# Last rows' norm scaled by a diagonal on TensorE, and an earlier start of the parameter loads, in a two-layer hybrid decoder kernel

## The chip, the cores and the metric

The kernel runs on one core of one Trainium2 chip. The metric is the device time in microseconds (us) of one execution, taken as the median of several runs. Engines are called by their names: TensorE (PE in the rows, PEld for its weight loads), VectorE (DVE), ScalarE (ACT), GpSimd (POOL) and SyncE (SP). DMAs are issued from the queues of SP, ACT and POOL.

## The reference

Two decoder layers work on x of 256 rows and 2048 columns, float32. Each layer multiplies x by one wide input matrix, feeds the product's column groups to three token mixers (a short convolution, latent attention with rotary positions, an RWKV-7 recurrence), concatenates their gated outputs and applies an output projection, a residual and a LayerNorm:

```python
for l in range(DEPTH):
    u = x @ w_in[l]
    (cb, cc, ch, cg, cq, ckv, kpe, mg, rcols, rg) = _split(u, IN_SIZES)
    ...
    mix = jnp.concatenate([y_conv, y_mla, y_rwkv], axis=-1)
    x = _layer_norm(DEEPNORM_ALPHA * x + mix @ w_out[l], ln_g[l], ln_b[l])
```

Here x is the input (1, 256, 2048), and the result has the same shape.

## The kernel before

**Arithmetic.** A float32 operand that feeds a large product is split into a high part (a cast on ScalarE) and a low part (a subtraction on VectorE), both in the type fp32r, and the product is summed from two or three fp32r matmuls. A few smaller products use plain float32 operands.

**Order.** The code emits the work group by group: for each layer the column groups of the input product in the order k, a, r, v, cq, cc and so on, then the attention products, then the output projection `out_proj`. The mixers are generators; `tick()` advances each of them by a step between blocks of a group's matmuls, so that their small instructions run beside TensorE's matmuls. A scheduler at compile time fixes each engine's order by simulated ready times and priorities; `after(a, b)` only says that a stands behind b in an engine's order. On the chip each engine runs its list in that order.

**The first group.** For layer 0 the group k is special (`wide_group`, `load_first`): x and the weights of k come together, in the blocks that `STEPS` lists as (first chunk, number of chunks) of the 16 chunks of 128 rows. Before, the blocks are 1, 1 and then seven times 2 chunks. A chunk is 384 KB. Each block is one DMA on SP's queue into a buffer named `first`, is split into high and low parts of x and of the weights, and gives 12 matmuls for each chunk into the accumulator `u_k`. Buffers of the kind that `first` uses are nine, and four of them hold x.

**Parameters.** `load_constants` starts the DMAs of the parameters `pars`, the constants `cs`, the positions and the matrix of ones on POOL's queue. They stand behind a one-element copy on GpSimd that reads a block of x, so that they start when that block has landed: before, the last one (k0 == 14). `load_params` (line 248) works out `pc` from `pars` with four small VectorE instructions for each layer. The step `shift_mix` (line 472) of the RWKV mixer needs `pc`: four times a ScalarE activation and a VectorE instruction read a quarter of the accumulator `u_k` and write `kx`.

**The second group.** Group a follows: eight blocks of weights `w_a` (4 chunks each), four for the accumulator `u_a` of half 0 and four for that of half 1. Accumulators come from `acc` (line 353), a pool of two buffers in PSUM. `u_k` and the first half of `u_a` hold both; the second half takes the one that the compile-time scheduler expects to be free first. The first half of `u_a` is evicted by a ScalarE copy and a VectorE addition (lines 455 and 456). `rope_tables` (line 262) makes sine and cosine tables from the positions meanwhile, with `Sin` activations on ScalarE.

**The output projection.** `out_proj` computes four groups g of 512 columns, for two halves h of 128 rows. The fourth group is computed in two parts i of 256 columns; in layer 0 the part i = 1 does h = 0, then `add` (VectorE reads the accumulator), then h = 1. Then `root(1)` works out the rows' `rstd` and the mean term, `turn_row` transposes the latter on TensorE (`cwt`, copied to `ct`), and `norm` adds the product of `ct` and `gr` (line 1295, `lw`) with one VectorE instruction for each group and starts the output DMA. In the last layer, groups 1, 2, 3 of the last 128 rows end the kernel. `keep_warm` gives TensorE twelve matmuls whose result nobody reads while VectorE works out `rstd`.

Of the kernel before, what the change touches and what calls it, by code (L numbers as in the profile page):

```python
# [10 lines left out]
F32 = mybir.dt.float32  # L11
# [6 lines left out]
P = 128  # L18
# [93 lines left out]
def hybrid_layers(ctx: ExitStack, tc: tile.TileContext, x, positions, xT, w_in, w_out, w_uq, w_ukv, par, wa_in, gb_in,  # L112
# [34 lines left out]
    def after(inst, earlier):  # L147

        tc.add_manual_dep(inst.ins, earlier.ins.name,
                          mybir.DependencyInfo(mybir.DependencyClass.NoSync, mybir.DependencyReason.DATA),  # L150
                          reason="loads no earlier than needed")
# [15 lines left out]
    def load_constants(x):  # L167

        last = G.tensor_copy(pars[0:1, 0, 0:1], x[0:1, 0:1])
        for to, src in ((pars, par), (cs, cst), (posi, positions[0:1, :].to_broadcast([P, S]))):  # L170
            load = nc.gpsimd.dma_start(to, src)
            after(load, last)
            last = load
        o32 = c4("ones32", (P, 2 * P))
        load = nc.gpsimd.dma_start(o32, sums)
        after(load, last)
        V.tensor_copy(ones, o32)
        loaded.append(load)

    def zeros(rows):  # L180

# [31 lines left out]
    xres = x  # L213
    xs = [pair(f"x0_{g}") for g in range(4)]

    STEPS = [(0, 1), (1, 1), (2, 2), (4, 2), (6, 2), (8, 2), (10, 2), (12, 2), (14, 2)]

    def load_first(k0, n):

        t = s8(f"first{k0}", (P, n, S + 512))  # L220
        in_turn(1, nc.sync.dma_start(t, xT[:, k0:k0 + n, :]))
        with tc.high_priority():
            to, at = xs[k0 // 4], k0 % 4
            split_in(to[:, 0, at:at + n, :], to[:, 1, at:at + n, :], t[:, :, 0:S])
        if k0 == 14:
            load_constants(t[:, 0, :])
        return t[:, :, S:].rearrange("p k (i c) -> p i k c", i=2)

# [19 lines left out]
    def load_params(l):  # L248
        pq = pars[:, l, :]
        pc = cp.tile([P, 29], F32, tag=f"pc{l}", name=f"pc{l}")  # L250
        V.tensor_scalar(pc[:, 0:13], pq[:, Q_MUR:Q_MUR + 13], -1.0, 1.0, ALU.mult, ALU.add)
        V.tensor_scalar(pc[:, 13:21], pq[:, Q_W0:Q_W0 + 8], 0.5, None, ALU.mult)
        V.tensor_scalar(pc[:, 21:25], pq[:, Q_KA:Q_KA + 4], 0.5, None, ALU.mult)
        V.tensor_scalar(pc[:, 25:29], pq[:, Q_KA:Q_KA + 4], -0.5, 1.0, ALU.mult, ALU.add)
        col = lambda j: pq[:, j:j + 1] if j < NQ else pc[:, j - NQ:j - NQ + 1]
        return dict(col=col, om=NQ - Q_MUR, hw=NQ + 13, ha=NQ + 17, hk=NQ + 21, ok=NQ + 25)

# [955 lines left out]
    def ln_rows(l):  # L1213

        t = sm.tile([P, 2, 16], F32, tag="lnp", name=f"lnp{l}", bufs=1)
        load = nc.gpsimd.dma_start(t, gbp[l])
        after(load, loaded[0])
        hi = sm.tile([P, 2, 16], F32R, tag="lnh", name=f"lnh{l}", bufs=1)
        lo = sm.tile([P, 2, 16], F32R, tag="lnl", name=f"lnl{l}", bufs=1)
        V.tensor_copy(hi, t)  # L1220
        V.tensor_tensor(lo, t, hi.bitcast(F32), ALU.subtract)
        rows = dr.tile([5, D], F32R, tag=f"lnr{l}", name=f"lnr{l}")
        for i, src in enumerate((hi[:, 0], lo[:, 0], hi[:, 0], hi[:, 1], lo[:, 1])):
            nc.gpsimd.dma_start(rows[i].rearrange("(p i) -> p i", p=P), src)
        return rows

    def out_proj(l, ms, xres, last, begin, lnr):
# [23 lines left out]
        def rows(g):  # L1251
            return xn[0, :, g * 512:(g + 1) * 512].rearrange("(h p) c -> p h c", p=P)
# [89 lines left out]
        for g in range(4):  # L1342
            xr = c4(f"xr{l}_{g}", (P, 2, 512))
            after(nc.scalar.dma_start(xr, xres[0, :, g * 512:(g + 1) * 512].rearrange("(h p) c -> p h c", p=P)), begin)
            zs.append(xr)
            gt = s4(f"gb{l}_{g}", (P, 2, 512))
            after(nc.scalar.dma_start(gt, gb_in[l:l + 1, :, g * 512:(g + 1) * 512].to_broadcast([P, 2, 512])), begin)
            gs.append(gt)
            if g < 3:
                pa = acc(f"po{l}_{g}")  # L1350
                po = [pa[:, h, :] for h in range(2)]
                for k0 in ORDER:
                    ws = [weights(f"wo{l}_{g}", k0 + k) for k in (0, 2)]
                    for h in range(2):
                        part(po, h, 512, ws)
                for h in range(2):
                    add(po[h], g, 0, 512, h, g)
                continue
            po, held = [], {}
            for i in range(2):  # L1360
                pa = acc(f"po{l}_{g}_{i}")
                po.append([pa[:, h, 0:256] for h in range(2)])
                held[i] = []
                for k0 in ORDER:
                    held[i].append(weights(f"wo{l}_3_{i}", k0))
                    if not last and i == 0:
                        for h in range(2):
                            part(po[i], h, 256, held[0][-1:])
                if not last and i == 0:
                    for h in range(2):  # L1370
                        add(po[i][h], g, 0, 256, h, 3)
            cts = []

            def turn_row(h):
                ct, m = row(h)
                cts.append(ct)
                return m

            first_rows = {AT[last][0]: lambda: turn_row(0),
                          AT[last][1]: lambda: [norm(0, g_, cts[0])[0] for g_ in range(4 if last else 1)][-1]}  # L1380
            for h in range(2):
                for i in range(2):
                    if not last and i == 0:
                        continue
                    part(po[i], h, 256, held[i], first_rows if h and i else {})
                    add(po[i][h], g, i * 256, 256, h, 3 + i)
                mark.setdefault(l + 1, []).append(root(h))
            if not last:
                xs += [pair(f"x{l + 1}_{g}") for g in range(1, 4)]
            keep_warm()  # L1390
            if last:
                turn_row(1)
                part1(256, 256)
                nc.scalar.dma_start(rows(0)[:, 1], zs[0][:, 1])
                for g_ in range(1, 4):
                    norm(1, g_, cts[1], ((0, 512),) if g_ < 3 else ((0, 256), (256, 256)))
            else:
                turn(1, 0, ((0, 2),))
                t = turn(0, 0, hold=mark[l + 1][1])
                after(part0(256, 256), mark[l + 1][1])  # L1400
                mark[l + 1][1] = t
                part1(256, 256)
                nc.gpsimd.dma_start(rows(0), zs[0])
                turn(1, 0, ((2, 2),))
                turn_row(1)
                run(rest(cts))
                tick()
# [60 lines left out]
```

## Time and profile before

| | us |
|---|---|
| median of 3 runs | 908.29 (908.03 to 909.82) |
| the profiled execution, its own time | 909.28 |
| its span in the trace | 907.5 |
| TensorE busy in the span | 893.1 |
| VectorE, ScalarE, GpSimd busy | 687.5, 486.1, 24.6 |

The profiled execution is one more execution beside the three. Its time is 1.8 us longer than the span, which runs from the first to the last event of the trace. Times in the rows count from the start of the span. "Busy" for TensorE holds pipelined matmuls, so 98% is not 98% of its peak rate; it says only that it was seldom without work.

### The profile page before, as it was taken

How to read it: one execution, taken by the hardware profiler on the slowest of the kernel's cores; microseconds unless marked ns; L12 is line 12 of the kernel's file. 1: busy time of each engine (PE TensorE's matmuls, PEld its weight loads, DVE VectorE, ACT ScalarE, POOL GpSimd, SP SyncE). 2: the span in 40 equal slices, each digit the busy share in tenths (PEclk: the TensorE clock that was granted, in tenths of full speed). 3: DMA queues.
4: the chain of work that ended last, by engine and by line, in shares of the span. 5: the costliest groups of instructions: out<-in, count | busy, mean ns of one | idle time of the engine just before them, and what ended most of it. 6: DMA issues, size and time to landing. Idle time of an engine off the chain costs nothing.

```text
span 907.5 us, 16003 instructions
## 1 busy us (share of the span) xinstructions
PE 893.1 (98%) x6314; PEld 786.7 (87%) x6314; DVE 687.5 (76%) x1166; ACT 486.1 (54%) x752; POOL 24.6 (3%) x47
## 2 busy tenths in 40 slices
PE   8899999999999999999999999999999999999996
PEld 8788888888889888888898888888888998988896
DVE  7677988986558987476775889799765699875665
ACT  6577546444447666544246874564444575765430
POOL 2120000000000000000020000000000000000000
PEclk9989999999999999999999999999999999999999
DMA  9755674666535654696576456646654456547832
GB/s 373 222 139 161 185 208 130 187 197 177 161 111 165 193 161 118 205 325 204 171 225 194 136 190 191 170 124 204 196 173 141 123 158 209 163 118 239 315 119 93
DMA packets 65100, 164.98 MB, mean 182 GB/s; under 512 B 15286, under 2 KB 23782, under 8 KB 65014
## 3 DMA queue, kind: packets, MB, share of 16 engines
q1 hardware_dynamic: 57264, 150.36, 54.4%
q10 hardware_dynamic: 5072, 9.57, 3.0%
q0 software_dynamic: 2688, 4.03, 1.6%
q8 instruction: 49, 0.80, 0.4%
q14 instruction: 27, 0.22, 0.1%
HBM read 158.61 MB, written 5.32 MB: 181 GB/s over the span
## 4 chain that ended last, share of the span: by engine, by line
PE 95%; DVE 2%; ACT 1%; DMA 1%; issue 0%; DVEq 0%; SPq 0%; ACTq 0%
PE po L341 7%; PE u_mg L441 7%; PE po L343 7%; PE po L342 6%; PE u_a L441 4%; PE u_cc L441 3%; PE u_cg L441 3%; PE u_mg L443 3%; PE u_v L441 3%; PE u_cb L441 3%; PE u_ch L441 3%; PE u_cq L441 3%; PE u_rg L441 3%; PE u_r L441 3%; PE u_rg L443 2%; PE u_cg L443 2%
## 5 line engine op out<-in xcount | busy, mean ns | idle before, releaser
L138 DVE TENSOR_TENSOR lo_wo<-w_wo,hi_wo 128x1024 fp32r<-128x1024 f32 x57 | 69.1, 1222 | 45.0 <-ACT hi_wo L138 44.1
L138 ACT CAST hi_wo<-w_wo 128x1024 fp32r<-128x1024 f32 x57 | 59.3, 1050 | 60.1 <-PE po L343 29.9
L441 PE MATMUL u_mg<-x,hi_mg 128*128 128x512 f32 x256 | 90.0, 396 | 0.0
L443 PE MATMUL u_mg<-x,lo_mg 128*128 128x256 f32 x256 | 71.4, 280 | 0.0
L441 PEld LDWEIGHTS u_mg<-x,hi_mg 128*128 128x128 f32 x256 | 47.9, 188 | 10.8
L441 PE MATMUL u_a<-x,hi_a 128*128 128x512 f32 x128 | 48.1, 415 | 3.1 <-DVE u_a L138 3.1
L443 PEld LDWEIGHTS u_mg<-x,lo_mg 128*128 128x128 f32 x256 | 48.3, 189 | 0.2
L341 PE MATMUL po<-hi_wo,ma 128*128 128x512 f32 (+1 forms) x128 | 46.7, 365 | 0.0
L343 PE MATMUL po<-hi_wo,ma 128*128 128x512 f32 (+1 forms) x128 | 46.5, 363 | 0.0
L342 PE MATMUL po<-lo_wo,ma 128*128 128x512 f32 (+1 forms) x128 | 46.4, 363 | 0.0
L138 ACT CAST hi_mg<-w_mg 128x1024 fp32r<-128x1024 f32 x32 | 33.6, 1049 | 23.8 <-PE u_mg L441 12.5
L441 PE MATMUL u_cc<-x,hi_cc 128*128 128x512 f32 x128 | 46.2, 403 | 0.0
L441 PE MATMUL u_cg<-x,hi_cg 128*128 128x512 f32 x128 | 46.0, 401 | 0.0
L441 PE MATMUL u_cq<-x,hi_cq 128*128 128x512 f32 x128 | 45.4, 395 | 0.0
L441 PE MATMUL u_ch<-x,hi_ch 128*128 128x512 f32 x128 | 45.3, 399 | 0.0
L441 PE MATMUL u_cb<-x,hi_cb 128*128 128x512 f32 x128 | 45.3, 399 | 0.0
L441 PE MATMUL u_v<-x,hi_v 128*128 128x512 f32 x128 | 45.3, 399 | 0.0
L441 PE MATMUL u_rg<-x,hi_rg 128*128 128x512 f32 x128 | 45.3, 394 | 0.0
L441 PE MATMUL u_r<-x,hi_r 128*128 128x512 f32 x128 | 45.1, 394 | 0.0
L138 DVE TENSOR_TENSOR lo_mg<-w_mg,hi_mg 128x1024 fp32r<-128x1024 f32 x32 | 38.8, 1222 | 6.0 <-ACT hi_mg L138 4.4
L343 PE MATMUL u_k<-x,lo_k 128*128 128x256 f32 x128 | 36.9, 288 | 0.8 <-DVE lo_k L138 0.8
L138 DVE TENSOR_TENSOR lo_rg<-w_rg,hi_rg 128x1024 fp32r<-128x1024 f32 x16 | 19.6, 1223 | 23.2 <-ACT hi_rg L138 23.2
(417 smaller groups left out, 2819.5 us busy)
## 6 DMA issues: line engine op xcount, KB each, us to landing
w_wo<-in_w_out_dram SPq DMA_DIRECT2D x64, 512.0 KB, 4.3
w_mg<-in_w_in_dram SPq DMA_DIRECT2D x32, 512.0 KB, 4.0
w_a<-in_w_in_dram SPq DMA_DIRECT2D x16, 512.0 KB, 4.5
w_r<-in_w_in_dram SPq DMA_DIRECT2D x16, 512.0 KB, 3.7
w_v<-in_w_in_dram SPq DMA_DIRECT2D x16, 512.0 KB, 3.7
w_cq<-in_w_in_dram SPq DMA_DIRECT2D x16, 512.0 KB, 3.8
w_cc<-in_w_in_dram SPq DMA_DIRECT2D x16, 512.0 KB, 4.0
w_ch<-in_w_in_dram SPq DMA_DIRECT2D x16, 512.0 KB, 3.7
```

The costliest lines, as they stand in the source:

```text
L138: inst = call(*args, **kwargs)
L341: m = T.matmul(o, lh, rh, start=first, stop=False, skip_group_check=True)
L342: T.matmul(o, lh, rl, start=False, stop=False, skip_group_check=True)
L343: T.matmul(o, ll, rh, start=False, stop=last, skip_group_check=True)
L441: T.matmul(ps[:, b, :].rearrange("p (i t) -> p i t", i=2), hi[:, k, c], x2, start=k0 + k == 0, stop=False, skip_group_check=True)
L443: T.matmul(ps[:, b, 0:S], lo[:, k, c], x2[:, 0, :], start=False, stop=k0 + k == NKC - 1, skip_group_check=True)
```

## The change

The change has four parts. (1) `STEPS` splits the block of chunks 2 and 3 into two blocks of one chunk. (2) The parameter loads hang on the block that begins at chunk 6 in place of the last one; the cast of the ones moves into `load_params`, and the small instructions of `load_params` are put behind the low part of the last block of k in VectorE's order. (3) In layer 0's output projection, half h = 1 of the part i = 1 gets an accumulator of its own. (4) In the last layer, groups 1 and 2 of the last rows are scaled by TensorE: ScalarE writes a 128x128 diagonal of `rstd`, a float32 matmul multiplies it by the rows, the product of `ct` and `gr` is added in the same PSUM buffer, and ScalarE copies the sum to SBUF. Group 3 is done as before, now ahead of them. The queues of three output DMAs change.

```diff
@@ load_constants
-        V.tensor_copy(ones, o32)
-        loaded.append(load)
+        loaded.extend((load, o32))
@@ blocks of the first group
-    STEPS = [(0, 1), (1, 1), (2, 2), (4, 2), (6, 2), (8, 2), (10, 2), (12, 2), (14, 2)]
+    STEPS = [(0, 1), (1, 1), (2, 1), (3, 1), (4, 2), (6, 2), (8, 2), (10, 2), (12, 2), (14, 2)]
@@ load_first
-        if k0 == 14:
+        if k0 == 6:
             load_constants(t[:, 0, :])
@@ load_params
-        V.tensor_scalar(pc[:, 0:13], pq[:, Q_MUR:Q_MUR + 13], -1.0, 1.0, ALU.mult, ALU.add)
...
+        vs = [V.tensor_scalar(pc[:, 0:13], pq[:, Q_MUR:Q_MUR + 13], -1.0, 1.0, ALU.mult, ALU.add),
...
+        if l == 0:
+            vs.append(V.tensor_copy(ones, loaded[1]))
+        for v in vs:
+            after(v, splits[len(STEPS) - 1][1])
@@ ln_rows
-        V.tensor_copy(hi, t)
+        after(V.tensor_copy(hi, t), splits[len(STEPS)][1])
@@ out_proj, the fourth group
                 pa = acc(f"po{l}_{g}_{i}")
-                po.append([pa[:, h, 0:256] for h in range(2)])
+                pb = pa if last or i == 0 else acc(f"po{l}_{g}_2")
+                po.append([pa[:, 0, 0:256], pb[:, 1, 0:256]])
@@ out_proj, the end of the last layer
             if last:
+                diag = sm.tile([P, P], F32, tag="rs", name="diag", bufs=2)
+                A.activation(diag, ident, AF.Identity, scale=rstd[:, 1:2])
+                scaled = []
+                for g_ in (1, 2):
+                    scaled.append(pm.tile([P, 512], F32, tag="m", name=f"zr{g_}"))
+                    T.matmul(scaled[-1], diag, zs[g_][:, 1, :], start=True, stop=False)
                 turn_row(1)
                 part1(256, 256)
-                nc.scalar.dma_start(rows(0)[:, 1], zs[0][:, 1])
-                for g_ in range(1, 4):
-                    norm(1, g_, cts[1], ((0, 512),) if g_ < 3 else ((0, 256), (256, 256)))
+                nc.sync.dma_start(rows(0)[:, 1], zs[0][:, 1])
+                norm(1, 3, cts[1], ((0, 256), (256, 256)))
+                for g_, pw in enumerate(scaled, 1):
+                    T.matmul(pw, cts[1], gr[:, g_ * 512:g_ * 512 + 512], start=False, stop=True)
+                    z = zs[g_][:, 1, :]
+                    A.copy(z, pw)
+                    (nc.scalar if g_ == 1 else nc.sync).dma_start(rows(g_)[:, 1], z)
```

## Rows read from the trace of the kernel before

**Rows 1.** Waits of TensorE, whole span: us in total, times, longest.

```profile
PE u_a L441 <- DVE u_a L138: 3.1, 1, 3.1
...
PE po L341 <- DVE xr L138: 0.5, 1, 0.5
```

**Rows 2.** TensorE's timeline around 41 us: start, us, engine, line, operation, idle before.

```profile
41.13 0.28 PE L443 MATMUL u_a<-x,lo_a 128*128 128x256 f32 x1
44.49 0.79 PE L441 MATMUL u_a<-x,hi_a 128*128 128x512 f32 x1 [3.08 <-DVE u_a L138]
```

**Rows 3.** Windows: stretch, length, busy per engine, granted clock, DMA share, GB/s.

```profile
44.00:50.00 6.00, 5.51 (x17) 4.74 (x18) 2.33 (x5) 4.51 (x9) 4.69 (x9) 0.50 0.60 124
...
30.27:59.42 29.15, 26.07 (x133) 22.34 (x132) 20.39 (x45) 20.38 (x29) 8.24 (x15) 0.88 0.66 166
482.40:505.84 23.44, 23.44 (x134) 20.27 (x133) 15.87 (x22) 17.53 (x29) 0.00 (x0) 1.00 0.62 180
```

**Rows 4.** VectorE's timeline, 32 to 45 us.

```profile
32.47 0.68 DVE L138 TENSOR_SCALAR pc<-pars 128x13 f32<-128x13 f32 x8
...
44.35 0.48 DVE L138 SCALAR_TENSOR_TENSOR kx<-u_k,pars,kx 128x255 f32<-128x255 f32 x1
```

**Rows 5.** ScalarE's timeline, 30 to 45 us (layer 0).

```profile
30.25 1.05 ACT L138 CAST hi_a<-w_a 128x1024 fp32r<-128x1024 f32 x1 [2.06 <-PE u_k L342]
...
33.80 0.47 ACT L138 ACTIVATE kx<-u_k,pc 128x256 f32<-128x256 f32 x1
...
42.28 0.58 ACT L138 COPY u_a<-u_a 128x512 f32<-128x512 f32 x1
...
43.65 1.28 ACT L138 ACT_TABLE_LOAD   x1
44.95 0.51 ACT L138 ACTIVATE sinT<-ang,cs 128x256 f32<-128x256 f32 x1
```

**Rows 6.** ScalarE's timeline at the same place in layer 1.

```profile
482.39 1.05 ACT L138 CAST hi_a<-w_a 128x1024 fp32r<-128x1024 f32 x1 [1.83 <-PE u_k L342]
483.34 0.47 ACT L138 ACTIVATE kx<-u_k,pc 128x256 f32<-128x256 f32 x1
```

**Rows 7.** Timeline of all engines, 7 to 10 us.

```profile
7.04 0.62 ACT L138 CAST x<-first 128x512 fp32r<-128x512 f32 x1 [0.97 <-DMA first<-in_xT_dram]
...
8.93 0.62 ACT L138 CAST x<-first 128x512 fp32r<-128x512 f32 x1 [0.31 <-DMA first<-in_xT_dram]
...
9.93 0.19 PEld L343 LDWEIGHTS u_k<-x,lo_k 128*128 128x128 f32 x1 [0.96 <-DVE lo_k L138]
```

**Rows 8.** GpSimd's timeline at 18 us.

```profile
18.40 0.93 POOL L169 COPY pars<-first 1x1 f32<-1x1 f32 x1 [3.56 <-DMA first<-in_xT_dram]
```

**Rows 9.** DMA queues, 10 to 28 us: queue, packets, MB, share.

```profile
q0 software_dynamic: 256, 0.70, 10.7%
...
ones<-in_sums_dram POOLq DMA_DIRECT2D x1, 128.0 KB, 6.3
```

**Rows 10.** TensorE's timeline at 316 us: float32 matmuls, two records each.

```profile
316.10 0.38 PE L1092 MATMUL sc<-kn,qn 128*128 128x128 f32 x2
316.32 0.39 PE L1094 MATMUL sc<-kpe,qp 128*128 128x128 f32 x2
```

**Rows 11.** Timeline of all engines from 899 us to the end.

```profile
899.07 0.16 DVE L138 SCALAR_TENSOR_TENSOR rstd<-nr,rstd 128x1 f32<-128x1 f32 x1
...
900.15 0.27 PE L1286 MATMUL cwt<-cs,cw 128*5 128x128 f32 x1 [0.99 <-DVE cw L138]
...
901.07 0.96 PE L1295 MATMUL lw<-gr,ct 5*128 5x512 f32 x4 [0.65 <-DVE ct L138]
901.60 2.19 DVE L138 SCALAR_TENSOR_TENSOR xr<-xr,rstd,lw 128x512 f32<-128x512 f32 x4 [0.59 <-PE lw L1295]
902.38 1.38 SPq L1298 DMA_DIRECT2D out_dram<-xr  x2
```

**Rows 12.** Windows at the end, columns as in rows 3.

```profile
903.20:905.40 2.20, 0.00 (x0) 0.00 (x0) 0.59 (x2) 0.00 (x0) 0.00 (x0) 0.65 0.99 354
```

More of the change, by code (lines that the diff above doesn't have):

```diff
@@ L250, in load_params @@
         pc = cp.tile([P, 29], F32, tag=f"pc{l}", name=f"pc{l}")
-        V.tensor_scalar(pc[:, 0:13], pq[:, Q_MUR:Q_MUR + 13], -1.0, 1.0, ALU.mult, ALU.add)
-        V.tensor_scalar(pc[:, 13:21], pq[:, Q_W0:Q_W0 + 8], 0.5, None, ALU.mult)
-        V.tensor_scalar(pc[:, 21:25], pq[:, Q_KA:Q_KA + 4], 0.5, None, ALU.mult)
-        V.tensor_scalar(pc[:, 25:29], pq[:, Q_KA:Q_KA + 4], -0.5, 1.0, ALU.mult, ALU.add)
+        vs = [V.tensor_scalar(pc[:, 0:13], pq[:, Q_MUR:Q_MUR + 13], -1.0, 1.0, ALU.mult, ALU.add),
+              V.tensor_scalar(pc[:, 13:21], pq[:, Q_W0:Q_W0 + 8], 0.5, None, ALU.mult),
+              V.tensor_scalar(pc[:, 21:25], pq[:, Q_KA:Q_KA + 4], 0.5, None, ALU.mult),
+              V.tensor_scalar(pc[:, 25:29], pq[:, Q_KA:Q_KA + 4], -0.5, 1.0, ALU.mult, ALU.add)]
+        if l == 0:
+            vs.append(V.tensor_copy(ones, loaded[1]))
+        for v in vs:
+            after(v, splits[len(STEPS) - 1][1])
         col = lambda j: pq[:, j:j + 1] if j < NQ else pc[:, j - NQ:j - NQ + 1]
```

## The prediction

> **What bounds the kernel now.** I read the waits of TensorE first, then the timeline around the longest of them, then windows over the same stage in both layers, and last the head and the tail. TensorE is busy 893.1 of 907.5 us, so a change can win in two ways only: by taking away one of TensorE's few waits, or by shortening the stretch after its last large matmul. The waits are a short list [rows 1]: one of 3.1 us before a matmul of `u_a`, one of 0.5 us in `po`, and a shorter one in the first group, which the timeline shows [rows 7]. All other engines work in TensorE's shadow.
>
> The longest wait is at 41.41 us, when the first half of `u_a` is done (41.13 + 0.28), and the second half begins at 44.49 [rows 2]. It needs one of the two accumulators. `u_k` is held until `kx` has read its last quarter, at 44.83 (44.35 + 0.48) [rows 4]; the first half of `u_a` is evicted a little earlier, and that releases TensorE. So `kx` is late. The reason stands in the order of VectorE and ScalarE: `pc` is worked out at 32.47 [rows 4], after which the first `kx` follows at 33.80, 3.55 us after the cast of the fourth `w_a` block at 30.25 [rows 5]. In layer 1, where `pc` has long been there, the same `kx` starts 0.95 us after the same cast (482.39, 483.34) [rows 6], one block earlier, and no wait for `u_a` stands there: there is one in the whole run [rows 1].
>
> The wait costs more than itself. During the idle stretch the granted clock falls to 0.50, the lower level of 1.2 GHz, and stays there through 44 to 50 us [rows 3]. The whole stage from the first matmul of `u_a` to `u_r` takes 29.15 us in layer 0 and 23.44 in layer 1, with TensorE busy throughout the latter at clock 1.00 [rows 3]: 5.7 us more for the same matmuls, 3.1 of them idle and 2.6 by the clock.
>
> **Part 1, smaller blocks.** The block of chunks 2 and 3 lands at 7.04, the next at 8.93 [rows 7]: 1.9 us for two chunks. Its low weights are ready only for the matmul at 9.93, which cost 0.96 us [rows 7]. From there to 30.27 TensorE does 166 matmuls of the group (192 less 26), 0.12 us each, so 1.45 us for a chunk. Split in two, chunk 2 lands half a block earlier, at about 6.1, and its split of half the size (some 1.5 us in place of the 2.9 from 7.04 to 9.93) is over by 7.7; TensorE asks for it at about 9.0. Chunk 3 lands at 7.04, is split by about 8.8 and asked for at 10.4. The block after it still lands at 8.93 and is split by 11.8, as before, just when TensorE, no longer held up, comes to its low part (11.9). So the gain is the whole 0.9, or 0.7 if that meeting misses. One more DMA on SP's queue costs nothing as long as the queue is ahead of the data, and it is: the casts wait for bytes, not for an issue.
>
> **Part 2, parameters.** Moved are the one-element copy (0.93 us on GpSimd) [rows 8], five DMAs on POOL's queue, four `pc` instructions for each layer and the cast of the ones. The copy now waits for the block at chunk 6, one behind that at chunk 4, so it runs at about 8.93 + 1.9 = 10.8 in place of 18.40, 7.6 us earlier. The DMAs follow, and the slowest row takes 6.3 us to land [rows 9], so all are there by about 20 us even with their issues in a row. The DMAs pass the last four blocks of x on SP's queue: 0.70 MB [rows 9], at the rate of the blocks (0.79 MB in 1.9 us) 1.7 us of delay at most. What hides it: a block of two chunks takes 2.9 us of matmuls and 1.9 us to land, so TensorE falls behind the data by 1 us a block. The block at chunk 10, the first that the DMAs can hold up, would be split by about 17.4 and is asked for at about 20.3. I cost the delay at nothing; without that cover it would be 1.7.
>
> `pc` then stands on VectorE behind the last low part of k, at about 21 us, and its eight instructions (0.68) [rows 4] fall into VectorE's idle time there. Queued behind them are the low parts of `w_a`, the first of which TensorE needs at about 29.4. With `pc` ready, `kx` can follow the fourth cast of `w_a` as in layer 1, one block (2.8 us) earlier. That frees `u_k` at about 44.83 - 2.8 - 0.9 = 41.1, against the end of the first half of `u_a` at 41.41 - 0.9 = 40.5: by layer 0's own pace 0.6 of waiting remains, and in layer 1 none does. I take layer 1's stage as the model, 29.15 down to 23.44, a gain of 5.7, less 0.2 for a remainder: 5.5. From both sides: nothing, if the order of `kx` does not move, and 5.7; if it moves, 5.1 to 5.7.
>
> **A table load in the way.** ScalarE loads a table set at 43.65 in 1.28 us, and the `Sin` follows at 44.95, 0.02 after it [rows 5]. With the positions there earlier, the scheduler may put this `Sin` between the third and the fourth `kx`, where it would hold `kx` up by 1.28 + 0.51 = 1.8 us. The Trainium skill, ScalarE: Activation LUTs, What ACT_TABLE_LOAD costs, has a switch of sets at 1283 ns for the load and about 1380 ns for a drain, 2.66 us in all. This trace agrees with the load and shows no drain beside it. By the page the hold-up would be 3.2 us and eat most of the 5.5.
>
> **Part 3, an accumulator of its own.** The wait of 0.5 us in `po` [rows 1] is TensorE's first matmul of h = 1, held by VectorE's reading of h = 0 from the same tile, and the code has one such place. With two tiles nothing is read there. The pool's other buffer is free by then, since the part i = 0 was added before. Gain 0.5 (0.3 if the new tile waits for something else).
>
> **Part 4, the tail.** `rstd` is ready at 899.23 [rows 11]. The diagonal has 128 columns; 256 take 0.47 on ScalarE [rows 5]; I take 0.4, so 899.7. The two matmuls are plain float32. No row has one of 512 columns. One of 128 is two records, and the next begins 0.22 later [rows 10]; four times that is 0.88, and 1.76 for both. From below, four `lw` matmuls in fp32r, 1536 columns, span 0.96 [rows 11], so 0.25 for a pass over 512 and 1.0 for four records; from above, 3.5 at the lower clock. I take 1.76, the same type. TensorE is then free at 901.45, and the transpose `cwt`, behind them in the program, moves from 900.15 to there, 1.3 later. `lw` followed 0.92 after `cwt`, partly because VectorE was busy then; with 0.6 it starts at 902.05, not 901.07. VectorE's first instruction came 0.53 after `lw` [rows 11], now at about 902.6. There the change takes off: VectorE does only group 3, about 0.85 of the 2.19 us, and ScalarE copies the two sums at 0.58 each [rows 5], from about 902.9 to 904.0. But the end is a matter of bytes: the first store, issued at 902.38, flows from 903.20, and the stores then run at 354 GB/s until 905.40 [rows 11, 12]. The same 0.79 MB starts at about 903.05 + 0.8 and needs its 2.2 us again, ending at 906.0. I price the part at +0.6. It is -0.1 if the scheduler puts `cwt` between the two matmuls, and +1.2 if ScalarE's store of group 3's second part stands between its copies and makes the last one wait.
>
> **Sum.** -0.9 - 5.5 - 0.5 + 0.6 = -6.3 us. The profiled execution took 909.28 (span 907.5 and 1.8 around it), so it would be 903.0; it lies 1.0 above the median of the runs, 908.29, so the median would be 902.0. With each term at its ends (5.1 to 5.7 for part 2) the net is -7.2 to -4.9: 901.1 to 903.4.
>
> **Rivals.** *The wait shrinks but stays.* The `Sin` with its table goes ahead of the fourth `kx`, or the scheduler again gives the second half of `u_a` the buffer of the first, which needs a copy of 0.58 and an addition before it is free. Then 1.5 to 3.3 us of the 5.5 remain: 903.5 to 905.3. For it speaks that in layer 1 `kx` and TensorE meet with nothing to spare, and layer 0 has the rope tables besides; against it, that ScalarE and VectorE both have idle stretches between the blocks of `w_a`. *The parameters don't matter.* If the simulated order leaves `kx` behind the fifth cast, the wait and the clock remain, and only 0.9 + 0.5 - 0.6 = 0.8 is won: 907.5. Against it: `pc` stands in the order where its data came, and the data come 7.6 us earlier. *Slower.* The nine small VectorE instructions now stand ahead of all low parts of `w_a`. If the loads on POOL's queue land late behind x, VectorE stops there. It decides from the point where they land after about 28 us: TensorE needs the first low part at 29.4, and it takes 1.2. Each us beyond costs one, and an idle stretch like that of [rows 2] brings the lower clock, 2.6 more; the later wait would be spared. Landing at 34 gives 5.8 + 2.6 on top of the forecast: 910.4. Against it: the slowest landed 6.3 us after its issue with the same queue full [rows 9].
>
> **Chances.** The forecast 0.56, the shrunken wait 0.25, no effect of the parameters 0.14, slower 0.05. A measurement here can tell about 0.2%, 1.8 us, from no change. The first two are faster by more than that (0.81), the third is within it (0.14), the last beyond it (0.05). The range takes in the forecast with its ends and the shrunken wait: 900.9 to 905.3. The forecast's own is 901.1 to 903.4.
>
> **What the profile would show.** Right: no wait of `u_a` on VectorE above 0.5 us and a granted clock of 1.00 from 35 to 60 us; `pc` near 21 us and the first `kx` within 1 us of the fourth cast of `w_a`; no wait near 9.9 and 442 us; the two float32 matmuls taking 1.7 to 1.8 us ahead of `cwt`, and the last bytes about 2.3 us after the first store of group 3 begins to flow. Wrong: `kx` still one block late, a table load between two `kx`, or a wait of VectorE on a DMA near 21 us.

## The result and the profile after

| | before | after |
|---|---|---|
| median of the runs, us | 909.06 (908.03 to 910.03, 4 runs) | 903.05 (902.96 to 903.51, 4 runs) |
| ratio, 95% interval | | 0.9935 [0.9918, 0.9952] |
| profiled execution: own time, span | 909.28, 907.5 | 903.07, 901.3 |

The change makes the kernel faster by 6.0 us in these runs, and the two profiled executions differ by 6.2. Predicted were 902.0 us and a range of 900.9 to 905.3. Line numbers of the kernel after are three higher than before from the matmul helpers on (L341 is L344, L441 is L444).

The waits of TensorE over the whole span of the kernel after (us in total, times, longest):

```profile
PE pzero L243 <- DVE zeror L138: 1.9, 1, 1.9
PE zr L1401 <- ACT diag L138: 0.6, 1, 0.6
PE pq L344 <- ACT vt L138: 0.5, 2, 0.2
PE xt L1310 <- PE pz L1342: 0.4, 1, 0.4
PE lw L1298 <- DVE ct L138: 0.4, 1, 0.4
```

The waits for `u_a` and in `po` [rows 1] are gone, and so is the one in front of chunk 2's low part [rows 7]. New is the wait of the diagonal's matmuls in the tail. The windows of the stage from `u_a` to `u_r`, kernel after, columns as in rows 3:

```profile
44.00:50.00 6.00, 6.00 (x35) 5.12 (x34) 4.15 (x6) 4.49 (x7) 0.53 (x2) 1.00 0.90 252
29.95:53.24 23.29, 23.29 (x133) 20.16 (x132) 19.30 (x34) 20.18 (x29) 5.32 (x10) 1.00 0.81 226
```

The stage is read from the first matmul of `u_a` with `lo_a`: one with `hi_a` runs ahead of it, in layer 0 at 27.30 among the matmuls of `u_k`. TensorE is busy throughout and the granted clock is 1.00, the upper level of 2.4 GHz, where [rows 3] have 0.50 and a stage of 29.15. Why it no longer waits stands in the timelines of GpSimd, VectorE and ScalarE, kernel after:

```profile
11.61 0.96 POOL L169 COPY pars<-first 1x1 f32<-1x1 f32 x1 [11.15 <-DMA first<-in_xT_dram]
...
15.19 0.54 POOL L1219 DMA_DIRECT2D lnp<-in_gbp_dram  x1
```

```profile
24.25 0.38 DVE L138 TENSOR_SCALAR pc<-pars 128x13 f32<-128x13 f32 x4
...
30.66 0.48 DVE L138 SCALAR_TENSOR_TENSOR kx<-u_k,pars,kx 128x255 f32<-128x255 f32 x1 [1.43 <-ACT kx L138]
```

```profile
30.15 0.47 ACT L138 ACTIVATE kx<-u_k,pc 128x256 f32<-128x256 f32 x1 [2.18 <-PE u_k L346]
30.52 1.04 ACT L138 CAST hi_a<-w_a 128x1024 fp32r<-128x1024 f32 x1
...
42.14 0.57 ACT L138 COPY u_a<-u_a 128x512 f32<-128x512 f32 x1
42.73 1.28 ACT L138 ACT_TABLE_LOAD   x1
44.03 0.51 ACT L138 ACTIVATE sinT<-ang,cs 128x256 f32<-128x256 f32 x1
```

The copy of one element runs 6.8 us earlier than in [rows 8], `pc` 8.2 us earlier than in [rows 4], and the first `kx` stands in front of the fourth cast of `w_a`, not 3.55 us behind it [rows 5]: it starts as soon as TensorE has finished `u_k`. The table load has not moved between two `kx`.

The tail of the kernel after, all engines, from the scaling of the diagonal on:

```profile
892.66 0.40 ACT L138 ACTIVATE diag<-cs,rstd 128x128 f32<-128x128 f32 x1 [0.95 <-DVE rstd L138]
...
893.12 1.98 PE L1401 MATMUL zr<-xr,diag 128*128 128x512 f32 x4 [0.56 <-ACT diag L138]
...
894.94 0.27 PE L1289 MATMUL cwt<-cs,cw 128*5 128x128 f32 x1
...
895.58 0.50 PE L1298 MATMUL lw<-gr,ct 5*128 5x256 f32 x2 [0.37 <-DVE ct L138]
...
896.00 0.87 DVE L138 SCALAR_TENSOR_TENSOR xr<-xr,rstd,lw 128x256 f32<-128x256 f32 x2 [0.47 <-PE lw L1298]
896.35 1.07 ACT L138 COPY xr<-zr 128x512 f32<-128x512 f32 x2 [3.28 <-PE zr L1407]
896.51 0.33 SPq L1301 DMA_DIRECT2D out_dram<-xr  x1
...
897.44 0.33 SPq L1410 DMA_DIRECT2D out_dram<-xr  x1
```

`lw` starts 3.11 us behind the start of the last `rstd` instruction (892.47), where it was 2.00 [rows 11]: the float32 matmuls hold TensorE for 1.8 us in front of the transpose `cwt`. The copies end 4.95 us behind that point, VectorE's four pieces ended 4.72 behind it before. The saved work buys back all but 0.23 us of the delay. The first store of group 3 goes out 4.04 us behind that point (896.51), before 3.31 (902.38).

**Where the time went, by landmarks of the two traces** ("the last `pz`" are the twelve matmuls of `keep_warm` behind the last products):

| stretch, us | before | after | difference | predicted |
|---|---|---|---|---|
| start to the first `u_a` matmul with `lo_a` | 30.17 | 29.95 | -0.22 | -0.9 |
| from there to the first of `u_r` | 29.22 | 23.29 | -5.93 | -5.5 |
| from there to the last `pz` matmuls | 837.19 | 836.74 | -0.45 | -0.5 |
| from there to the end of the span | 10.92 | 11.32 | +0.40 | +0.6 |
| sum | 907.5 | 901.3 | -6.20 | -6.3 |

The sum is nearly that of the prediction, the terms less so (their differences nearly cancel), and the median lies 1.0 above the forecast. The experiments are about these differences.

### The profile page after: what moved, and what is told of

The parts are those of the page before. It is cut to its first block, busy times and chain, and to the rows that moved or that the text cites. A ratio compares the mean times of both kernels' runs of the same rounds, so it can differ in the third digit from the quotient of the medians.

```text
span 901.3 us, 16025 instructions
## 1 busy us (share of the span) xinstructions
PE 892.5 (99%) x6318; PEld 785.6 (87%) x6318; DVE 686.6 (76%) x1166; ACT 487.7 (54%) x757; POOL 25.0 (3%) x47
## 4 chain that ended last, share of the span: by engine, by line
PE 96%; DVE 2%; ACT 1%; DMA 1%; issue 0%; SPq 0%; ACTq 0%
PE u_mg L444 7%; PE po L344 7%; PE po L345 7%; PE po L346 7%; PE u_cc L444 3%; PE u_cg L444 3%; PE u_mg L446 3%; PE u_ch L444 3%; PE u_a L444 3%; PE u_cb L444 3%; PE u_v L444 3%; PE u_cq L444 3%; PE u_r L444 3%; PE u_rg L444 3%; PE u_rg L446 2%; PE u_cg L446 2%
## 5 line engine op out<-in xcount | busy, mean ns | idle before, releaser
L444 PE MATMUL u_mg<-x,hi_mg 128*128 128x512 f32 x256 | 90.0, 396 | 0.0
L444 PEld LDWEIGHTS u_mg<-x,hi_mg 128*128 128x128 f32 x256 | 47.9, 188 | 10.8
L344 PE MATMUL po<-hi_wo,ma 128*128 128x512 f32 (+1 forms) x128 | 46.7, 365 | 0.0
L444 PE MATMUL u_cc<-x,hi_cc 128*128 128x512 f32 x128 | 46.2, 403 | 0.0
L444 PE MATMUL u_cg<-x,hi_cg 128*128 128x512 f32 x128 | 46.0, 401 | 0.0
L444 PE MATMUL u_a<-x,hi_a 128*128 128x512 f32 x128 | 45.4, 398 | 0.0
L444 PE MATMUL u_cq<-x,hi_cq 128*128 128x512 f32 x128 | 45.4, 395 | 0.0
L444 PE MATMUL u_ch<-x,hi_ch 128*128 128x512 f32 x128 | 45.3, 399 | 0.0
L444 PE MATMUL u_r<-x,hi_r 128*128 128x512 f32 x128 | 45.3, 396 | 0.0
L444 PE MATMUL u_cb<-x,hi_cb 128*128 128x512 f32 x128 | 45.3, 399 | 0.0
L444 PE MATMUL u_v<-x,hi_v 128*128 128x512 f32 x128 | 45.3, 399 | 0.0
L444 PE MATMUL u_rg<-x,hi_rg 128*128 128x512 f32 x128 | 45.3, 394 | 0.0
```

Of the source, the lines that this page charges most:

```text
L344: m = T.matmul(o, lh, rh, start=first, stop=False, skip_group_check=True)
L444: T.matmul(ps[:, b, :].rearrange("p (i t) -> p i t", i=2), hi[:, k, c], x2, start=k0 + k == 0, stop=False, skip_group_check=True)
```

## The experiments

Each part of the change was made alone (on one chip, 908.13 us for the kernel before, 906.53 to 911.84, 29 runs), then the tail was varied and the load moved without its orders (another chip, 908.26, 906.73 to 909.07, 9 runs), then parts were taken out of the changed kernel (a third, 908.84, 907.16 to 909.91, 15 runs). The median of all 57 runs of the kernel before is 908.22. This table has the same landmarks in each profiled execution ("after" is a second one of the changed kernel); "GB/s" is the rate at 5 to 6 us, "chunk 4" the start of the cast of that block of x. The spans are given to 0.1 us, so the tail is good to about 0.05.

| kernel | median, us | GB/s | chunk 4 | first `lo_a` | stage | middle | tail |
|---|---|---|---|---|---|---|---|
| before | | 442 | 8.93 | 30.17 | 29.22 | 837.19 | 10.92 |
| part 2 alone | 903.72 | 412 | 9.02 | 30.27 | 23.29 | 837.51 | 10.93 |
| part 1 alone | 908.25 | 252 | 9.92 | 30.15 | 29.04 | 837.22 | 10.99 |
| part 3 alone | 907.40 | 424 | 9.03 | 30.28 | 28.05 | 836.46 | 10.91 |
| part 4 alone | 908.50 | 418 | 8.99 | 30.22 | 27.76 | 837.24 | 11.28 |
| load without orders | 904.88 | 418 | 9.01 | 31.83 | 23.18 | 837.20 | 10.89 |
| fill | 907.95 | 418 | 8.88 | 30.12 | 26.56 | 838.60 | 10.92 |
| after | 903.19 | 292 | 9.71 | 29.96 | 23.29 | 836.76 | 11.29 |
| after less part 1 | 903.77 | 412 | 9.85 | 31.14 | 23.28 | 836.89 | 11.29 |
| after less part 3 | 904.07 | 280 | 10.36 | 30.61 | 23.29 | 837.63 | 11.37 |
| after less part 4 | 902.85 | 313 | 9.59 | 29.85 | 23.29 | 836.68 | 11.08 |
| after, `cwt` first | 903.31 | 286 | 9.67 | 29.92 | 23.29 | 837.13 | 11.26 |

**Part 2 alone.**

```
-        if k0 == 14:
+        if k0 == 6:
             load_constants(t[:, 0, :])
...
+            vs.append(V.tensor_copy(ones, loaded[1]))
+        for v in vs:
+            after(v, splits[len(STEPS) - 1][1])
...
+        after(V.tensor_copy(hi, t), splits[len(STEPS)][1])
```

> The kernel before with the second part alone: the parameters asked for behind the block of chunks 6 and 7, the orders behind the last x block and the first wk block, and the copy of ones moved. Blocks of x, accumulator and tail as before. Theory (the early parameters let `kx` be cast one block earlier, and that takes the 3.08 us wait and the half clock behind it): the first wait for `kx` is gone, the stretch from the first matmul of `u_a` to that of `u_r` falls from about 29.2 to about 23.3 us, and the time is 5.5 to 6.0 us below the kernel before. Rival (the gain needs the split block of chunks 2 and 3 too, since the casts reach `kx` in time only when all of them start earlier): a wait of 0.5 us or more stays in front of the second half of `u_a`, the clock falls behind it, and the time is 2 to 4 us below.

Measured: 903.72 us (903.50 to 904.59, 5 runs), ratio 0.9954 [0.9942, 0.9966]; 4.4 below the median beside it. The window of its stage:

```profile
30.27:53.56 23.29, 23.29 (x133) 20.18 (x132) 19.30 (x34) 20.18 (x29) 5.27 (x9) 1.00 0.80 217
```

The wait is gone and the stage is 23.29, as in the whole change, so the rival falls: blocks of one chunk are not needed for it. The stage is worth the expected 5.9 against the profiled execution of before, but the medians differ by 4.4 only, less than the 5.5 to 6.0 expected. The fill below says why.

**Part 1 alone.**

```
-    STEPS = [(0, 1), (1, 1), (2, 2), (4, 2), (6, 2), (8, 2), (10, 2), (12, 2), (14, 2)]
+    STEPS = [(0, 1), (1, 1), (2, 1), (3, 1), (4, 2), (6, 2), (8, 2), (10, 2), (12, 2), (14, 2)]
```

> The kernel before with the first part alone: chunks 2 and 3 of x in blocks of one. Theory now (a wait of 0.96 us in front of chunk 2 goes, but the matmuls reach their full rate later and the blocks from chunk 3 on land some 0.8 us later, so most of it is given back): the first matmul of `u_a` starts 0.1 to 0.4 us earlier, and the time is 0.1 to 0.4 us below the kernel before. The predicted term: 0.9 us earlier and 0.9 us below. Rival (the late blocks move the whole head, and the wait for `kx` grows because the casts are later): no change, or up to 0.5 us above.

Measured: 908.25 (906.10 to 909.75, 12 runs), ratio 0.9997 [0.9986, 1.0009]: nothing that can be told. TensorE's record in front of chunk 2's low part in the kernel before:

```profile
9.93 0.39 PE L343 MATMUL u_k<-x,lo_k 128*128 128x256 f32 x1 [0.76 <-DVE lo_k L138]
```

TensorE's timeline of the kernel with part 1 around chunk 4, ScalarE's before it, and the window of 5 to 6 us:

```profile
11.76 0.28 PE L342 MATMUL u_k<-x,hi_k 128*128 128x256 f32 x1
12.80 0.39 PE L343 MATMUL u_k<-x,lo_k 128*128 128x256 f32 x1 [0.76 <-DVE lo_k L138]
```

```profile
9.92 0.62 ACT L138 CAST x<-first 128x512 fp32r<-128x512 f32 x1 [0.92 <-DMA first<-in_xT_dram]
```

```profile
5.00:6.00 1.00, 1.00 (x4) 0.71 (x4) 0.95 (x3) 0.94 (x3) 0.00 (x0) 1.00 1.04 252
```

The 0.76 us in front of chunk 2's low part now stand in front of chunk 4's, to the hundredth. The block of chunk 4 is cast at 9.92 instead of 8.93 [rows 7], because the transfers slow down for a moment: 252 GB/s where the kernel before moves 442. This dip (252 to 313 GB/s) is in all six executions profiled with the split block (280 in the first of the changed kernel), and in none of the eight without (406 to 442, the fill's first try below among them), so it comes with the split. The DMA engines' share is no lower, 1.04: 97 packets kept the engines busy as long as 151 did in the microsecond before (4 to 5 us, also 1.04), and the packets are no larger. What in the transfers makes them slow, the profile does not show.

**Part 3 alone.**

```
-                po.append([pa[:, h, 0:256] for h in range(2)])
+                pb = pa if last or i == 0 else acc(f"po{l}_{g}_2")
+                po.append([pa[:, 0, 0:256], pb[:, 1, 0:256]])
```

> The kernel before with the third part alone: an accumulator of its own for the second half of `po`. Theory: the wait of TensorE for the copy of `po` in the first layer is gone and nothing is late in its place: 0.4 to 0.5 us below the kernel before. Rival (the stage behind it is bound elsewhere): within 0.2 us of it.

Measured: 907.40 (905.63 to 908.84, 12 runs), ratio 0.9991 [0.9981, 1.0001]; 0.73 below. The interval reaches 1, so the times alone do not settle it. The middle of the trace is 0.73 shorter, which is more than the wait of 0.5; the run that takes the part out again shows why.

**Part 4 alone**, the diff of the tail as in the change.

> The kernel before with the fourth part alone: groups 1 and 2 of the last rows scaled by a diagonal on TensorE and copied by ScalarE. Theory (the float32 matmuls stand in front of the transpose of `cwt` on TensorE, so that `ct` and every closing matmul are later, and the copies of ScalarE take longer than VectorE's): 0.3 to 0.6 us above the kernel before, with the span's end 11.1 to 11.3 us behind the last large matmul where it was 10.8. Rival (the tail of the changed kernel looks long only because other parts moved its start): within 0.2 us of the kernel before, or below it.

Measured: 908.50 (906.93 to 909.72, 11 runs), ratio 1.0006 [0.9997, 1.0014]; 0.37 above by the medians, and 0.36 longer from the last `pz` to the end in the trace. The time alone does not settle it, but the trace does: the five executions with this tail in its order have 11.28 to 11.37 there, and the seven in the table with the tail of before 10.89 to 11.08.

**The changed kernel without part 4.**

> The changed kernel with its fourth part undone: the end of the last rows' norm as it was before, the other three parts in. Theory (the fourth part costs 0.4 us): 902.6 to 902.8 us, 0.3 to 0.5 below the changed kernel, and 6.4 to 6.8 below the kernel before. Rival (the fourth part costs nothing or gains): 903.0 us or more.

Measured: 902.85 (902.67 to 903.53, 5 runs), ratio 0.9943 [0.9931, 0.9956]. TensorE and VectorE in its tail:

```profile
893.39 0.27 PE L1289 MATMUL cwt<-cs,cw 128*5 128x128 f32 x1 [0.99 <-DVE cw L138]
...
894.32 0.96 PE L1298 MATMUL lw<-gr,ct 5*128 5x512 f32 x4 [0.65 <-DVE ct L138]
894.85 2.19 DVE L138 SCALAR_TENSOR_TENSOR xr<-xr,rstd,lw 128x512 f32<-128x512 f32 x4 [0.59 <-PE lw L1298]
```

`lw` starts 4.50 us behind the start of the last `pz` (889.82), in the changed kernel 5.60 (889.98 to 895.58). This is the lowest median of all, by 0.2 to 0.3 under the changed kernel. The runs overlap and were made on different chips, so by times alone it is not shown to be the faster one.

**The transpose of `cwt` ahead of the diagonal matmuls**, in the changed kernel.

```
                 scaled = []
+                turn_row(1)
                 for g_ in (1, 2):
                     scaled.append(pm.tile([P, 512], F32, tag="m", name=f"zr{g_}"))
                     T.matmul(scaled[-1], diag, zs[g_][:, 1, :], start=True, stop=False)
-                turn_row(1)
```

> The changed kernel with the transpose of `cwt` issued ahead of the two diagonal matmuls on TensorE. Theory (the 1.98 us of float32 matmuls stand in front of the transpose and make `ct` late): `cwt` starts 0.3 us or more earlier in reference to the last large matmul, VectorE's copy `ct` too, and the time is 0.2 to 0.5 us below the changed kernel. Rival (the end is set by the diagonal matmuls and by ScalarE's two copies, which are not earlier): within 0.1 us of the changed kernel, since the closing matmuls still stand behind the diagonal ones.

Measured: 903.31 (902.97 to 903.93, 5 runs), ratio 0.9946 [0.9934, 0.9959]: the rival. Its trace is also 0.37 longer in the middle, a stretch that the edit does not touch, so the tail is what decides. All engines:

```profile
893.91 0.27 PE L1289 MATMUL cwt<-cs,cw 128*5 128x128 f32 x1 [0.99 <-DVE cw L138]
894.02 1.95 PE L1402 MATMUL zr<-xr,diag 128*128 128x512 f32 x4
...
894.50 0.27 DVE L138 CAST ct<-cwt 5x128 fp32r<-5x128 f32 x1
...
895.89 0.50 PE L1298 MATMUL lw<-gr,ct 5*128 5x256 f32 x2
```

`ct` is ready 1.1 us before TensorE is free, and yet `lw` starts 5.55 behind the last `pz`, where it was 5.60. The float32 matmuls delay the closing ones wherever `cwt` stands, so my theory that the order was at fault falls.

**The load without its orders**: of part 2 only the line `if k0 == 6`, in the kernel before.

> The kernel before with one line of the second part: the parameters asked for behind the block of chunks 6 and 7; no orders added, and the copy of ones where it was. Theory (the load alone is what is late): the casts of `kx` are still earlier by some 3 us, the wait is gone, and the time is 5.0 to 6.0 us below. Rival (without the orders the small copies and VectorE's waits for the parameters stand among the casts of x or in front of `kx`): a part of the wait stays or matmuls of `u_k` or `u_a` wait for a cast of x, and the time is 1 to 4 us below; above the kernel before only if VectorE stops for more than 3 us on a load.

Measured: 904.88 (904.83 to 905.42, 5 runs), ratio 0.9965 [0.9951, 0.9978]: 3.4 below the kernel before, as the rival gave, and 1.2 above part 2 whole. VectorE's timeline, and TensorE's behind it:

```profile
17.76 0.47 DVE L138 TENSOR_SCALAR pc<-pars 128x13 f32<-128x13 f32 x5 [4.04 <-DMA pars<-in_par_dram]
```

```profile
20.22 0.38 PE L343 MATMUL u_k<-x,lo_k 128*128 128x256 f32 x1 [0.97 <-DVE lo_k L138]
```

Without the orders `pc` stands among the splits of x, and VectorE stops for 4.04 us with three blocks of x behind it. The first `u_a` matmul with `lo_a` comes 1.56 us later than with the orders (31.83, 30.27). The wait for `kx` is gone all the same.

**The fill, first try**: 11 matmuls of 512 columns into an unread tile, issued in front of the second half of `u_a`, without an order.

> The kernel before, with 11 more matmuls of 512 columns on TensorE in front of the second half of `u_a` in layer 0, into a tile that nobody reads: they fill the 3.08 us wait and leave it in place. Theory (half of the gain is the wait itself and the other half the clock that falls behind it): the granted clock stays at 1.00 through 41 to 55 us, the stretch from `u_a` to `u_r` falls from 29.2 to 26.4 to 26.8 us, and the time is 2.4 to 2.8 us below the kernel before. Rival (the clock falls for another reason than the idle stretch, or what comes behind is late as well for the casts): no change, or up to 0.3 us above.

Measured: 911.91 (911.43 to 912.61, 5 runs), ratio 1.0042 [1.0029, 1.0055]. It tells nothing on the question: the matmuls ran at 7.42 us, among the first of `u_k`, and delayed the head. The table leaves this run out.

**The fill, in its place**: 12 matmuls, ordered.

```
+            if (l, name, i) == (0, "a", 1):
+                pf = pm.tile([P, 512], F32, tag="m", name="pfill")
+                for _ in range(FILL):
+                    fill = T.matmul(pf, xs[0][:, 0, 0, 0:P], xs[0][:, 0, 0:2, :], start=True, stop=True)
+                    after(fill, m)
...
+                        if fill is not None:
+                            after(m, fill)
```

> The kernel before with 12 more matmuls of 512 columns, into a tile that nobody reads, ordered behind the last matmul of the first half of `u_a` and in front of the first of the second half: TensorE works through the wait for `kx`, and the wait is not shortened. Theory (of the second part's gain one share is the wait of 3.1 us itself, the other the half clock behind it, whose length differs from run to run): the granted clock is 1.00 from 41 to 55 us, the stretch from the first `u_a` matmul with `lo_a` to the first of `u_r` is 26.3 to 26.7 us in place of 27.8 to 29.2, the median is 1.3 to 2.2 us below the kernel before, and the runs lie closer together than its 2 to 5 us. Rival (the clock falls whatever TensorE does there, or the gain behind it is hidden by casts that are late anyway): within 0.5 us of the kernel before, with a fall of the clock or a new wait behind the fill.

Measured: 907.95 (907.30 to 909.02, 11 runs), ratio 0.9991 [0.9983, 1.0000]; 0.9 below, less than the 1.3 to 2.2 expected. TensorE's timeline of this kernel, then its windows:

```profile
41.20 2.89 PE L440 MATMUL pfill<-x 128*128 128x512 f32 x12
44.45 0.50 PE L448 MATMUL u_a<-x,hi_a 128*128 128x512 f32 x1 [0.36 <-DVE u_a L139]
```

```profile
44.00:50.00 6.00, 5.64 (x32) 4.86 (x32) 2.67 (x6) 5.25 (x9) 4.72 (x9) 1.00 0.63 125
30.12:56.68 26.56, 26.20 (x145) 22.33 (x144) 20.14 (x46) 20.80 (x33) 9.15 (x15) 1.00 0.72 183
```

The second half of `u_a` begins at 44.45, as before (44.49), but at clock 1.00, and the stage is 26.56, as expected. This splits it: 26.56 less 23.29 is 3.27 for the wait, and what a stage with the wait takes above 26.56 is the clock. In the four profiled executions of the table with the bare wait that is 2.66 (before), 2.48, 1.49 and 1.20. The same two windows of the kernel with part 4 alone:

```profile
44.00:50.00 6.00, 5.46 (x24) 4.75 (x24) 2.48 (x6) 5.42 (x9) 4.66 (x8) 0.72 0.62 124
30.22:57.98 27.76, 24.69 (x133) 21.22 (x132) 20.39 (x45) 20.39 (x29) 9.22 (x15) 0.94 0.70 175
```

The stop is the same, yet the clock is back at its upper level by 48 us, where before it was 0.50 until past 50 [rows 3]. So the length of the fall differs from execution to execution. The profiled execution of before holds a long one (mean granted clock 0.994) and lies 1.06 above the median of all its runs (909.28, 908.22). Its other runs go the same way: of the 53 made beside the experiments, the ten with a mean clock of 0.994 have a median of 909.3 us, the nine with 0.997 one of 906.8, and those between (0.995 and 0.996) 908.1 and 908.2.

Of the 2.66 that the fill saves in the trace, 1.41 are given back further on: all but 0.14 of it lies between the first `u_cq` and the first `u_cc` matmul (31.14 us, before 29.87), where TensorE has no more idle time than before but the `pg` matmuls stand in another order among those of `u_cq`. I take that for a side effect of this kernel's order and did not try it further, so the time of the run is no price of the clock; the stage is.

**The changed kernel less part 1, less part 3, and as it is**, on one chip (the first two with the diffs above turned round).

> The changed kernel with its first part undone (chunks 2 and 3 of x in one block again). Theory from the run with the first part alone (the wait of 0.76 us in front of chunk 2 is moved to chunk 4 and not removed): a wait of 0.5 to 0.8 us in front of chunk 2's low part, none in front of chunk 4's, and the time within 0.3 us of the changed kernel. The prediction's own term: 0.9 us above it.

> The changed kernel with its third part undone (both halves of `po` in one accumulator again). Theory: the wait of 0.5 us of TensorE for the copy of `po` is back, and the time is 0.4 to 0.6 us above the changed kernel. Rival (the wait is made good behind it): within 0.2 us.

> The changed kernel as it is, on the same chip as the three runs beside it. Theory: 902.9 to 903.2 us, and 5.0 to 5.4 us below the kernel before, which is less than the 6.2 us between the two profiled executions since that of the kernel before held a longer stretch of half clock than most of its runs. Rival (the profiled execution of before was an ordinary one): 6.0 us or more below.

Measured: 903.77 (903.20 to 904.37), 904.07 (903.63 to 904.85) and 903.19 (902.96 to 904.24), 5 runs each; ratios 0.9945 [0.9933, 0.9958], 0.9949 [0.9937, 0.9962] and 0.9943 [0.9930, 0.9957]. Part 1 is worth 0.6 by the medians, with runs that overlap. Without it the head was 1.2 later in this trace, but there already the first two-chunk block was late (cast at 8.00, in before at 7.04 [rows 7]), which no other kernel without the split in the table shows (7.00 to 7.15). The medians of the first `lo_a` over all executions are the fairer measure: 29.96 with the split (six), 30.25 without it (six, the load without orders left out), so 0.3. Part 3 is worth 0.9 by the medians and 0.87 in the middle of the trace, of which the landmarks from `po` to the next `u_k` hold 0.77 (0.76 between before and part 3 alone). TensorE's timeline there, without part 3:

```profile
436.32 0.28 PE L346 MATMUL po<-wlwo,ma 128*128 128x256 f32 x1
437.11 0.39 PE L344 MATMUL po<-hi_wo,mc 128*128 128x256 f32 x1 [0.51 <-DVE xr L138]
437.33 0.28 PE L345 MATMUL po<-lo_wo,mc 128*128 128x256 f32 x1
```

The list says a wait of 0.51, but the starts are 0.79 apart where they are 0.12 in a run of such matmuls, and the next start is 0.22 behind where it would be 0.12: 0.67 and 0.10, together 0.77. The idle time is counted from the modelled end of the last matmul, and that lies 0.16 behind the moment at which the next could have started.

The changed kernel as it is gives 5.65 us by the medians and 5.2 by the ratio: the second lies within the 5.0 to 5.4 expected, the first above it, and both below the rival's 6.0.

## Why the prediction was right, and where it was off

**The mechanism held.** Early parameters let `kx` start before the fourth cast of `w_a`, the wait goes and the clock stays up. Part 2 alone gives the stage of 23.29, no remainder, so the term was 5.93 and not 5.5 against this profiled execution. Of the 0.43, 0.2 are the remainder that did not come. The rest is a reading: the two stretches that gave 5.7 [rows 3] are not over the same matmuls (133 and 134). Layer 1's holds the first one with `hi_a`, which in layer 0 ran at 27.30. From its first `lo_a` on layer 1 takes 23.23 us (482.54 to 505.77), so layer 1 was the right model. The fill shows both shares that the prediction read from the windows: 3.27 by the stop (3.1 predicted), 2.66 by the clock (2.6).

**The step that failed is the last one, from the profiled execution to the median.** The sum gave 903.0 for the profiled execution, and 903.07 came. Then 1.0 was taken off because the profiled execution lay 1.0 above the median. That 1.0 was a long stretch of half clock, which is in the term of part 2 already; with the wait gone the changed kernel has no such stretch, and its profiled execution lies at its median (903.07, 903.05). The loss was subtracted twice. Against 908.22 the change is worth 5.0 to 5.2. That the sum itself came out within 0.1 is partly luck: part 1 gave 0.7 less than predicted, part 2 0.4 more in its stage but 0.3 less behind it, part 3 0.3 more and part 4 cost 0.2 less.

**Part 1 was mis-sized: 0.9 predicted, 0.22 in the trace, about 0.3 over all of them.** The prediction let the block of chunk 4 land at 8.93 as before, and its "meeting" with TensorE at 11.9 hung on that. The block is 0.7 to 1.4 later than that in every execution with chunks 2 and 3 split. The casts wait for bytes and not for an issue, as it said, but the bytes themselves come more slowly. So the wait moves to chunk 4, and the head follows that one block. In all six executions with the split the first `lo_a` comes 20.23 to 20.26 us behind the cast of chunk 4's block. In the six of the table without it (the load without orders left out) it comes 23.12 to 23.14 behind that of chunk 2's. By that distance, with the block at 8.93 the head would have ended at 29.18 (an estimate), a gain of 1.0, so the size was right but for the 0.76 by which the block was late. In the changed kernel no wait is listed there, since its matmuls came to their full rate at 7.1 us and not 6.2. But two starts in front of chunk 4's low part stand 0.41 apart, where matmuls at the full rate start 0.12 apart:

```profile
12.17 0.28 PE L345 MATMUL u_k<-x,hi_k 128*128 128x256 f32 x1
12.58 0.39 PE L346 MATMUL u_k<-x,lo_k 128*128 128x256 f32 x1
```

**Part 2's surroundings.** The copy of one element was put at 10.8 and ran at 11.61. `pc` was put near 21 and stands at 24.25. The last block of x is cast at 21.51 against 18.37, 3.1 later, but that is no miss of the bound of 1.7 us: part 2 alone has it at 19.41, 1.0 later, and part 1 alone at 20.48, 2.1 later, a delay that the prediction did not look for. The cover named for it, TensorE falling behind the data by 1 us a block, held: no wait is listed in that group, so it costs nothing. In the u_r stage behind it part 2 gives back 0.3 (first `u_r` to first `u_v` 24.45, before 24.17). Nothing predicted that, the load without orders does not have it (24.17), and I did not follow it. The table load stayed behind the copy of `u_a`; the fear of it between two `kx` was unfounded in this order, and the activation again stands 0.02 us behind it (44.03). The drain that the Trainium skill, ScalarE: Activation LUTs, What ACT_TABLE_LOAD costs, adds to a switch of sets shows in neither trace.

**Part 3 was mis-sized: 0.5 predicted, 0.76 or 0.77 in two pairs of traces**, by reading the wait and not the distance of the starts.

**Part 4 was right in sign and near in size: +0.6 predicted, +0.40 in the trace.** Two float32 matmuls hold TensorE for 1.82 (893.12 to 894.94), predicted 1.76; `lw` is 1.11 later against `rstd`, predicted 0.98. The end was to follow from the first store of group 3 alone, 0.67 later; that store went out 0.73 later, but the end came only 0.40 later, so it is not set by the first store alone. The tail is longer in every trace that has this part, and taking `cwt` ahead of the float32 matmuls does not mend it.

**The rival on the slower side was real, but not here.** VectorE does stop on the parameter loads when the orders are left out: 4.04 us at 13.7. It came among the splits of x and not behind them, where TensorE had some cover. The medians put its cost, and so the worth of the orders, at 1.2.

## What to carry to other kernels

An idle stretch of TensorE is priced by the stage, not by the wait alone: here 3.3 us of stop cost 1.2 to 2.7 us more by the half clock, and that share differs from run to run (a median of 909.3 us for runs with a mean clock of 0.994, of 906.8 for those with 0.997). A gain worked out from one profiled execution must not be carried to the median if the very loss that is removed is what set that execution apart. And a wait that goes away in a pipeline of transfers is gone only if the next blocks come no later: follow the arrival of every block behind the edit, not only that of the one that was late.

## What the runs showed of the hardware

Splitting one transfer of 768 KB in two of 384 KB, on the same queue, brought a slow microsecond in each of six executions: 252 to 313 GB/s at 5 to 6 us, against 406 to 442 in eight without. The DMA engines' share was no lower for it (1.05 in the changed kernel, 1.06 before). And the granted clock of 0.50 behind the same stop of TensorE lasted from 6.8 us (before) down to 3.4 (part 4 alone), by the windows of 1 us from 43 to 51; the profile does not show what ends it. The kernel before ran from 906.5 to 911.8 us in 57 runs, those without the stop within 1.3 us each, though in five to nine runs only; with the stop filled they ran within 1.7 us (11 runs).
